# Bidirectional SSD mixer: decay exponents on 128 rows, C B masked 256 columns at a time, weighing on ScalarE

## The chip, the core and the metric

The kernel runs on one core of a Trainium2 chip. The metric is the device time of one execution in microseconds (us), lower is better. A core has TensorE (PE; matmuls into PSUM), VectorE (DVE), ScalarE (ACT), GpSimd (POOL) and SyncE (SP, which here issues the loads).

## What is computed

One encoder layer on 256 tokens of width 2048, in float32: a mixer, a gated conv feed-forward part, and a gated per-layer embedding, each between RMS norms. The mixer projects the normed input once with w_in into z, xbc, dt and u; the pooling half maps u; the SSD half is a bidirectional state-space scan with 16 heads in two groups, chunks of 128 tokens, and B and C of 128 states for each group. The change lies in the scan:

```python
dt = softplus(dt_raw + dt_bias)          # a column of its own for each direction
acum = cumsum(dt * a)
decay = exp(where(causal, acum[l] - acum[s], -inf))
cb = C[l] . B[s]                         # for each group
y_diag = einsum(cb, decay, xs * dt)      # within a chunk of 128
y_off = C . h_in * exp(acum)             # from the other chunk
y = y_fwd + flip(y_bwd) + xs * d_skip
```

## The kernel before, in words

Tokens form two chunks of 128 (t = 0, 1). Matrix products keep float32 accuracy by splitting each operand into a high half, a rounded copy (line 149, ScalarE, for weights), and a low half, the rest (line 150, VectorE); each product is then three fp32r matmuls: high-high, high-low, low-high. Weights come from HBM as 1 MB tiles (`raw`, 3 buffers); `whi` and `wlo` (lines 145 and 146) have 5 buffers each for the halves.

The mixer runs in this order. The projection onto dt and u (`dtu`, lines 399 to 436). Then three slabs of xbc, 512 columns each, feature-major: `xbc(2)` (B and C), `xbc(0)` and `xbc(1)` (xs), four units of w_in each. After a slab: scaling by rows (`times_rows`, line 367), a convolution of five taps (`conv`, lines 378 and 384), and SiLU (lines 598 and 600). Then z, token-major, eight units of two 128-row tiles (line 683). Then the norm of y, and the output projection `wo`.

The small work of the scan is laid between the units: `work` is a list of job lists, and `aside()` takes one list after every unit (lines 189 to 194). The tile framework then puts the instructions into the engines' queues when the program is built, by its own reckoning of what is ready, with the source's order as priority. So a queue's order is fixed before the run, but isn't the source's word for word. Each engine takes its queue in order.

The jobs that matter here:

- `seg_sums` (line 521): cumulative sums of the decays by a matmul, and from them `seg_w` and `seg_x`, two pages of which 64 rows are used: heads and a selection of ones, so that a matmul gives acum[l] - acum[s] for four heads at once. Half of the rows are filled early (lines 446 and 448), half here (532 and 533).
- `seg(i)`, i = 0 to 7 (line 535): two matmuls, one for each direction, `seg_w` (64 rows, 128 columns) by `seg_x` (64 rows, 512 columns), into two `misc` PSUM tiles; ScalarE copies one (541), VectorE takes the minimum of the two (542), ScalarE the exponential (543), into `ee[t]`. Where s <= l the minimum picks the forward exponent, elsewhere the backward one.
- `cb(cv, g)` (line 572): C B for one group, 256x256 in four blocks; the two diagonal blocks are multiplied by 0.25 and two masks into `cbm[0]` and `cbm[1]` (581, VectorE), the off-diagonal ones by 0.25 into `cbm[2]` (583, ScalarE).
- `weigh(t, g)` (line 603): w = cbm[0] dt_fwd + cbm[1] dt_bwd for the eight heads of a group: the second product by GpSimd (606), the first one and the sum by VectorE, 128 columns an instruction (611); then `ee` is multiplied by w (615). `w` is a `mid` tile (1024 columns, 3 buffers, shared with the tiles of the convolution).
- `far` and `skip` (lines 620, 625): xs scaled by the decays to the chunk's end, and xs times d_skip, on GpSimd.
- `mix(t, g)` (line 629): the part from the other chunk (`yo`, with `cbm[2]`), and eight matmuls of `ee` by `xs` (`yd`), into y. It needs the weighed `ee`.
- `pool_map` (line 559): matmuls of the pooling half, fp32, 128 rows.

`page` is a pool of 13 tiles of 2048 columns that nearly everything large shares (normed input: four pages until z ends; `ee` 2, `cath1`, `catl1`, `cbm`, `xs`, `y`, `xd` 2, and so on); a tile waits until a page is free. `misc` is two PSUM banks, `main` six.

Of the kernel before, what the change touches and what calls it, by code (L numbers as in the profile page):

```python
# [11 lines left out]
F32 = mybir.dt.float32  # L12
F32R = mybir.dt.float32r
AF = mybir.ActivationFunctionType
ALU = mybir.AluOpType

P = 128
L = 256
# [3 lines left out]
H = 16  # L22
# [29 lines left out]
def build(nc, a, out):  # L52
# [5 lines left out]
    with tile.TileContext(nc) as tc, \  # L58
# [11 lines left out]
        def page(name, dtype=F32):  # L70
            return gp.tile([P, 2048], dtype, tag="pg", bufs=13, name=name)

        def mid(name, dtype=F32):
            return gp.tile([P, 1024], dtype, tag="mid", bufs=3, name=name)

        def tiny(name, n=2):
            return sp.tile([P, n], F32, tag="tiny", bufs=40, name=name)
# [4 lines left out]
        def misc(name):  # L82
            return pc.tile([P, 512], F32, tag="misc", name=name)

        def mm(o, lhsT, rhs, start, stop):
            nc.tensor.matmul(o, lhsT, rhs, start=start, stop=stop, skip_group_check=True)  # L86
# [28 lines left out]
        def load(dst, src, ahead=False):  # L115

            with tc.issue_after(last["dma"]) if last and not ahead else nullcontext():
                return ins(nc.sync.dma_start(dst, src))
# [11 lines left out]
        mask = small[:, 80:592].rearrange("p (m f) -> p m f", m=4)  # L130

        low, among, four = small[:64, 592:593], small[:64, 593:597], small[:64, 597:601]
# [210 lines left out]
        def row_rstd(name, src):  # L343

            r = []
            for t in range(2):
                q = tiny(f"{name}q{t}", 1)
                junk = page(f"{name}j{t}")
                nc.scalar.activation(junk, src[t], AF.Square, accum_out=q)
                r.append(rms(f"{name}{t}", [q], 1.0 / D))  # L350
            return r
# [86 lines left out]
        with tc.issue_after(half[0]), tc.issue_after(half[1]):  # L438
            xs_ = [page(f"x{t}") for t in range(2)]
            for t in range(2):  # L440
                load(xs_[t], x[t * P:(t + 1) * P, :])
            rx = row_rstd("rx", xs_)
            seg_w = page("seg_w", F32R)[:64, :].rearrange("p (a q s) -> p a q s", a=4, q=4)
            seg_x = page("seg_x", F32R)[:64, :].rearrange("p (a i l) -> p a i l", a=4, i=4)
            for a_ in range(4):
                nc.scalar.activation(seg_w[:32, a_], four[:32].unsqueeze(2).to_broadcast([32, 4, P]), AF.Copy,
                                     scale=-1.0)
                nc.scalar.copy(seg_x[32:, a_], among[32:].unsqueeze(2).to_broadcast([32, 4, P]))
            aneg = ep.tile([P, 32], F32, name="aneg")
            nc.scalar.activation(aneg, alog, AF.Exp)  # L450
            nc.gpsimd.tensor_scalar(aneg, aneg, -1.0, None, op0=ALU.mult)


            pt = page("pt")[:, :512].rearrange("p (k t) -> p k t", k=2)
            load(pt, a["p_t"])
            half_up = cp.tile([P, 1], F32, name="half_up")
            nc.gpsimd.memset(half_up, 0.5)
            pth = cp.tile([P, 2, L], F32R, name="pth")
            ptl = cp.tile([P, 2, L], F32R, name="ptl")
            nc.scalar.copy(pth, pt)  # L460
            nc.vector.tensor_sub(ptl, pt, pth.bitcast(F32))
# [8 lines left out]
        dt = ep.tile([P, 2, 32], F32, name="dt")  # L470
        ut = page("u")
        for t in range(2):
# [3 lines left out]
                                    op0=ALU.mult)  # L476
# [44 lines left out]
        def seg_sums():  # L521

            cps = misc("cps")
            for a_ in range(4):
                mm(cps[:64, a_ * P:(a_ + 1) * P], da4[:, a_ // 2, a_ % 2].rearrange("p r h -> p (r h)"),
                   mask[:, 3 * (a_ % 2), :], True, True)
            hi, c = page("seg_h", F32R)[:64, :512], page("seg_c")[:64, :512]
            nc.scalar.copy(hi, cps[:64, :])
            nc.vector.scalar_tensor_tensor(c, hi.bitcast(F32), low, cps[:64, :], op0=ALU.mult, op1=ALU.add)
            c4 = c.rearrange("p (a l) -> p a l", a=4)  # L530
            for i in range(4):
                nc.scalar.activation(seg_x[:32, :, i, :], c4[:32], AF.Copy, scale=among[:32, i:i + 1])
                nc.scalar.activation(seg_w[32:, :, i, :], c4[32:], AF.Copy, scale=four[32:, i:i + 1])

        def seg(i):
            t, q = divmod(i, 4)
# [29 lines left out]
                put(cat(8 + 2 * g + d), ps[:, d * L:(d + 1) * L], vec(V_PS + 2 * g + d))  # L566


        cbm = page("cbm")[:, :1536].rearrange("p (m g s l) -> p m g s l", m=3, g=2, s=2)
        xs = page("xs")  # L570

        def cb(cv, g):
            ps = misc(f"cb{g}")
            for s in range(2):
                mm(ps[:, s * L:(s + 1) * L], cv[:, g * L + s * P:g * L + (s + 1) * P],
                   cv[:, (2 + g) * L:(3 + g) * L], True, True)
            for s in range(2):
                dg = ps[:, s * L + s * P:s * L + (s + 1) * P]
                og = ps[:, s * L + (1 - s) * P:s * L + (2 - s) * P]
                for d in range(2):  # L580
                    nc.vector.scalar_tensor_tensor(cbm[:, d, g, s, :], dg, 0.25, mask[:, d, :],
                                                   op0=ALU.mult, op1=ALU.mult)
                nc.scalar.activation(cbm[:, 2, g, s, :], og, AF.Copy, scale=0.25)

        def xs_turn(cv, slab):
            for t in range(2):
# [15 lines left out]

        def weigh(t, g):

            w = mid(f"w{t}{g}")
            nc.gpsimd.tensor_tensor(w.rearrange("p (h l) -> p h l", h=8),
                                    cbm[:, 1, g, t, :].unsqueeze(1).to_broadcast([P, 8, P]),
                                    dt[:, t, H + 8 * g:H + 8 * g + 8].unsqueeze(2).to_broadcast([P, 8, P]),
                                    op=ALU.mult)
            for h in range(8):  # L610
                nc.vector.scalar_tensor_tensor(w[:, h * P:(h + 1) * P], cbm[:, 0, g, t, :],
                                               dt[:, t, 8 * g + h:8 * g + h + 1], w[:, h * P:(h + 1) * P],
                                               op0=ALU.mult, op1=ALU.add)
            es = ee[t][:, g * 1024:(g + 1) * 1024]
            nc.vector.tensor_mul(es, es, w)

        def by_head(ap_, n=H):
            return ap_.rearrange("p (h c) -> p h c", h=n)
# [10 lines left out]
        def mix(t, g):  # L629
            c0 = t * 1024 + g * 512  # L630
            s = 1 - t
            po = misc(f"yo{t}{g}")
            mm(po, cbm[:, 2, g, s, :], xd[s][:, g * 512:(g + 1) * 512], True, True)
            tm = mid(f"ym{t}{g}")[:, :512]
            nc.vector.tensor_tensor(by_head(tm, 8), by_head(po, 8),
                                    dec[:, 2 + s, 8 * g:8 * g + 8].unsqueeze(2).to_broadcast([P, 8, 64]), op=ALU.mult)
            nc.gpsimd.tensor_add(y[:, c0:c0 + 512], y[:, c0:c0 + 512], tm)
            pd = misc(f"yd{t}{g}")
            for h in range(8):
                mm(pd[:, h * 64:(h + 1) * 64], ee[t][:, (8 * g + h) * P:(8 * g + h + 1) * P],  # L640
                   xs[:, c0 + h * 64:c0 + (h + 1) * 64], True, True)
            nc.vector.tensor_add(y[:, c0:c0 + 512], y[:, c0:c0 + 512], pd)

        def job(f, *args):
            return lambda: f(*args)

        xd = {}
        work.extend([
            [],
            [job(pool_mix, 0), job(pool_mix, 1)],  # L650
            [job(pool_mix, 2), job(pool_mix, 3), job(decays), job(seg_sums)],
            [job(seg, 0), job(seg, 1)],
        ])
# [1 line left out]
        work.extend([  # L655
            [job(seg, 2), job(pool_map, 0), job(pool_map, 1)],
            [job(cb, bc, 0), job(cb, bc, 1), job(seg, 3)],
            [job(seg, 4), job(weigh, 0, 0), job(pool_map, 2)],
            [job(seg, 5), job(weigh, 0, 1), job(pool_map, 3)],
        ])  # L660
        xa = xbc(0)
        work.extend([
            [job(seg, 6)],
            [job(seg, 7), job(weigh, 1, 0)],
            [job(xs_turn, xa, 0), job(weigh, 1, 1)],
            [],
        ])
        xb = xbc(1)
# [1 line left out]


        work.extend([
            [],
            [],
            [],
            [job(xs_turn, xb, 1)],
            [job(far, 1), job(skip, 0), job(far, 0), job(skip, 1)],
            [job(mix, 0, 0)],
            [job(mix, 0, 1), job(mix, 1, 0)],
            [job(mix, 1, 1)],  # L680
# [89 lines left out]
        h = [page(f"h{t}") for t in range(2)]  # L770
# [116 lines left out]
        for half in range(2):  # L887
# [10 lines left out]
            for t in range(2):  # L898
                for n, (o, c0) in enumerate(columns(acc[t])):
# [6 lines left out]
                    if end:  # L906
# [3 lines left out]
                                                   op0=ALU.add, op1=ALU.mult)  # L910
                    q = tiny(f"gq{t}{half}{n}", 1)
# [60 lines left out]
```

## Time and profile before

| | us |
|---|---|
| median of 3 runs | 1136.15 (1134.97 to 1136.28) |
| the profiled execution | 1134.8 |
| its span, first to last instruction | 1132.7 |
| busy: TensorE | 1115.6 (98%) |
| busy: VectorE | 801.1 (71%) |
| busy: ScalarE | 612.0 (54%) |
| busy: GpSimd | 79.7 (7%) |

The granted TensorE clock is 0.997 of full speed over the span. The profile is one execution. Its page gives busy times, the chain of work that ended last, and groups of instructions; views of the trace give instructions in order of time, waits, and busy times by window. In the trace xbc(2) begins at 52.4 us, xbc(0) ends about 117, z begins at 148.1 and the output projection at 203.8. A row's shape `64*128 64x512` reads: the loaded operand has 64 rows and 128 columns, the moving one 64 rows and 512 columns. Records of matmuls overlap, since they are pipelined: the spacing of their starts is the rate, not their duration. Tile names in rows are those of the program without numbers: `xb_0l` is a low half of an xbc slab's weights, `z_1h` a high half of z's.

### The profile page before, as it was taken

How to read it: one execution, taken by the hardware profiler on the slowest of the kernel's cores; microseconds unless marked ns; L12 is line 12 of the kernel's file. 1: busy time of each engine (PE TensorE's matmuls, PEld its weight loads, DVE VectorE, ACT ScalarE, POOL GpSimd, SP SyncE). 2: the span in 40 equal slices, each digit the busy share in tenths (PEclk: the TensorE clock that was granted, in tenths of full speed). 3: DMA queues.
4: the chain of work that ended last, by engine and by line, in shares of the span. 5: the costliest groups of instructions: out<-in, count | busy, mean ns of one | idle time of the engine just before them, and what ended most of it. 6: DMA issues, size and time to landing. Idle time of an engine off the chain costs nothing.

```text
span 1132.7 us, 15349 instructions
## 1 busy us (share of the span) xinstructions
PE 1115.6 (98%) x6049; PEld 969.4 (86%) x6049; DVE 801.1 (71%) x1067; ACT 612.0 (54%) x837; POOL 79.7 (7%) x91
## 2 busy tenths in 40 slices
PE   9999999999999999999999999999999999999996
PEld 9998888888788888888888888888888888887885
DVE  6659995754866665665756666668988998898574
ACT  6846543554664545454544545454665666667462
POOL 0201105200110000000000000000000000002001
PEclk9999999999999999999999999999999999999998
DMA  9942276556456555655555555657466656665752
GB/s 357 377 148 75 90 260 227 175 177 197 147 185 193 192 194 192 196 187 186 186 187 188 188 191 193 196 190 227 153 221 217 204 173 222 189 210 159 230 179 74
DMA packets 129591, 219.03 MB, mean 193 GB/s; under 512 B 3696, under 2 KB 96752, under 8 KB 128624
## 3 DMA queue, kind: packets, MB, share of 16 engines
q1 hardware_dynamic: 129232, 217.70, 58.5%
q8 instruction: 47, 0.77, 0.3%
q10 hardware_dynamic: 288, 0.36, 0.1%
q14 instruction: 24, 0.20, 0.0%
HBM read 215.95 MB, written 2.10 MB: 192 GB/s over the span
## 4 chain that ended last, share of the span: by engine, by line
PE 94%; DVE 3%; ACT 1%; POOL 1%; issue 1%; DMA 0%; POOLq 0%; DVEq 0%; ACTq 0%
PE va L86 22%; PE ga L86 21%; PE dna L86 17%; PE woa L86 8%; PE gt L86 7%; PE xbc L86 5%; PE dtu L86 4%; PE z L86 4%; PE dns L86 3%; DVE h L751 1%; PE pw L86 1%; PE yd L86 0%; PE seg L86 0%; DMA dtur<-w_in 0%; PE mx L86 0%
## 5 line engine op out<-in xcount | busy, mean ns | idle before, releaser
L86 PE MATMUL ga<-wox,ug_0h 128*128 128x512 f32 x352 | 88.4, 391 | 0.0
L86 PE MATMUL ga<-wox,ug_1h 128*128 128x512 f32 x352 | 87.6, 390 | 0.0
L86 PE MATMUL va<-wox,uv_0h 128*128 128x512 f32 x352 | 87.5, 391 | 0.0
L86 PE MATMUL va<-wox,uv_1h 128*128 128x512 f32 x352 | 86.9, 389 | 0.0
L86 PEld LDWEIGHTS va<-wox,uv_1h 128*128 128x128 f32 x352 | 66.1, 188 | 13.7
L86 PEld LDWEIGHTS ga<-wox,ug_1h 128*128 128x128 f32 x352 | 65.8, 188 | 13.6
L86 PEld LDWEIGHTS va<-wox,uv_0h 128*128 128x128 f32 x352 | 64.7, 188 | 12.5
L86 PEld LDWEIGHTS ga<-wox,ug_0h 128*128 128x128 f32 x352 | 64.5, 188 | 12.2
L86 PE MATMUL dna<-dn_0h,hs 128*128 128x512 f32 x248 | 74.7, 389 | 0.0
L86 PE MATMUL dna<-dn_1h,hs 128*128 128x512 f32 x248 | 74.6, 389 | 0.0
L792 POOL TENSOR_TENSOR fc<-fc,rfb 128x1024 f32<-128x1024 f32 x11 | 26.7, 2426 | 439.1 <-ACT fc L791 439.1
L86 PEld LDWEIGHTS dna<-dn_0h,hs 128*128 128x128 f32 x248 | 46.5, 188 | 9.7
L86 PEld LDWEIGHTS dna<-dn_1h,hs 128*128 128x128 f32 x248 | 46.6, 188 | 9.7
L86 PE MATMUL ga<-wox,ug_1l 128*128 128x256 f32 x352 | 50.3, 284 | 0.0
L86 PE MATMUL ga<-wox,ug_0l 128*128 128x256 f32 x352 | 49.5, 283 | 0.0
L86 PE MATMUL va<-wox,uv_1l 128*128 128x256 f32 x352 | 49.4, 283 | 0.0
L86 PE MATMUL va<-wox,uv_0l 128*128 128x256 f32 x352 | 49.2, 283 | 0.0
L86 PEld LDWEIGHTS ga<-wox,ug_0l 128*128 128x128 f32 x352 | 46.8, 191 | 1.7
L86 PEld LDWEIGHTS va<-wox,uv_0l 128*128 128x128 f32 x352 | 46.7, 191 | 1.7
L86 PEld LDWEIGHTS ga<-wox,ug_1l 128*128 128x128 f32 x352 | 45.7, 192 | 0.2
L384 DVE SCALAR_TENSOR_TENSOR fc<-gr,vt,fc 128x255 f32<-128x255 f32 x88 | 40.3, 481 | 7.7 <-ACT fc L378 7.0
L86 PEld LDWEIGHTS va<-wox,uv_1l 128*128 128x128 f32 x352 | 45.4, 192 | 0.0
(1078 smaller groups left out, 2800.9 us busy)
## 6 DMA issues: line engine op xcount, KB each, us to landing
dn0r<-w_ffn_down SPq DMA_DIRECT2D x22, 1024.0 KB, 5.6
dn1r<-w_ffn_down SPq DMA_DIRECT2D x22, 1024.0 KB, 5.6
zr<-w_in SPq DMA_DIRECT2D x8, 1024.0 KB, 5.4
wo0r<-w_out SPq DMA_DIRECT2D x8, 1024.0 KB, 5.7
wo1r<-w_out SPq DMA_DIRECT2D x8, 1024.0 KB, 5.5
gt0r<-w_ple_gate SPq DMA_DIRECT2D x8, 1024.0 KB, 6.3
gt1r<-w_ple_gate SPq DMA_DIRECT2D x8, 1024.0 KB, 5.5
dtur<-w_in SPq DMA_DIRECT2D x14, 528.0 KB, 8.9
```

The lines of the kernel that those rows point to most:

```text
L86: nc.tensor.matmul(o, lhsT, rhs, start=start, stop=stop, skip_group_check=True)
L384: nc.vector.scalar_tensor_tensor(o[:, lo:hi], i[:, lo + d:hi + d], vec(wcol + j * wstep + f), o[:, lo:hi], op0=ALU.mult, op1=ALU.add)
L751: nc.vector.scalar_tensor_tensor(h[t][:, s], mg[t][:, s], r[t], h[t][:, s], op0=ALU.mult, op1=ALU.add)
L792: nc.gpsimd.tensor_tensor(cv.rearrange("p (f t) -> p f t", f=4), cv.rearrange("p (f t) -> p f t", f=4), rfb.unsqueeze(1).to_broadcast([P, ...
```

## The change

Three edits in the scan. First, `seg_w` and `seg_x` keep all 128 rows: two GpSimd memsets set rows 64 to 127 to zero, and the seg matmuls, whose source line doesn't change, contract over 128 rows. Second, `cb` copies the whole 256 columns for each s (512 in all) by one ScalarE instruction, scaled by 0.25, into `cbs`, and VectorE multiplies a diagonal block by both masks at once, 256 columns an instruction; the off-diagonal blocks are read from `cbs`. Third, `weigh` makes both products on ScalarE, one activation for each head and direction with dt as its scale, into the two halves of a page; VectorE adds the halves and multiplies `ee`. The four weighings move: the first from xbc(0) to the third unit of xbc(1), the others from xbc(0) and xbc(1) into z.

```diff
-            seg_w = page("seg_w", F32R)[:64, :].rearrange("p (a q s) -> p a q s", a=4, q=4)
-            seg_x = page("seg_x", F32R)[:64, :].rearrange("p (a i l) -> p a i l", a=4, i=4)
+            seg_w, seg_x = page("seg_w", F32R), page("seg_x", F32R)
+            for blank in (seg_w, seg_x):
+                nc.gpsimd.memset(blank[64:, :].bitcast(F32), 0.0)
+            seg_w = seg_w.rearrange("p (a q s) -> p a q s", a=4, q=4)
+            seg_x = seg_x.rearrange("p (a i l) -> p a i l", a=4, i=4)
...
-                nc.scalar.copy(seg_x[32:, a_], among[32:].unsqueeze(2).to_broadcast([32, 4, P]))
+                nc.scalar.copy(seg_x[32:64, a_], among[32:].unsqueeze(2).to_broadcast([32, 4, P]))
...
-                nc.scalar.activation(seg_w[32:, :, i, :], c4[32:], AF.Copy, scale=four[32:, i:i + 1])
+                nc.scalar.activation(seg_w[32:64, :, i, :], c4[32:], AF.Copy, scale=four[32:, i:i + 1])
...
-        cbm = page("cbm")[:, :1536].rearrange("p (m g s l) -> p m g s l", m=3, g=2, s=2)
+        cbm = page("cbm")
+        cbs = cbm[:, 1024:].rearrange("p (g s l) -> p g s l", g=2, s=2)
+        cbm = cbm[:, :1024].rearrange("p (m g s l) -> p m g s l", m=2, g=2, s=2)
...
+            nc.scalar.activation(cbs[:, g].rearrange("p s l -> p (s l)"), ps, AF.Copy, scale=0.25)
             for s in range(2):
-                dg = ps[:, s * L + s * P:s * L + (s + 1) * P]
-                og = ps[:, s * L + (1 - s) * P:s * L + (2 - s) * P]
-                for d in range(2):
-                    nc.vector.scalar_tensor_tensor(cbm[:, d, g, s, :], dg, 0.25, mask[:, d, :],
-                                                   op0=ALU.mult, op1=ALU.mult)
-                nc.scalar.activation(cbm[:, 2, g, s, :], og, AF.Copy, scale=0.25)
+                nc.vector.tensor_mul(cbm[:, :, g, s, :], mask[:, :2, :],
+                                     cbs[:, g, s, s * P:(s + 1) * P].unsqueeze(1).to_broadcast([P, 2, P]))
...
-            w = mid(f"w{t}{g}")
-            nc.gpsimd.tensor_tensor(w.rearrange("p (h l) -> p h l", h=8),
-                                    cbm[:, 1, g, t, :].unsqueeze(1).to_broadcast([P, 8, P]),
-                                    dt[:, t, H + 8 * g:H + 8 * g + 8].unsqueeze(2).to_broadcast([P, 8, P]),
-                                    op=ALU.mult)
-            for h in range(8):
-                nc.vector.scalar_tensor_tensor(w[:, h * P:(h + 1) * P], cbm[:, 0, g, t, :],
-                                               dt[:, t, 8 * g + h:8 * g + h + 1], w[:, h * P:(h + 1) * P],
-                                               op0=ALU.mult, op1=ALU.add)
+            w = page(f"w{t}{g}")
+            for d in range(2):
+                for h in range(8):
+                    nc.scalar.activation(w[:, d * 1024 + h * P:d * 1024 + (h + 1) * P], cbm[:, d, g, t, :], AF.Copy,
+                                         scale=dt[:, t, d * H + 8 * g + h:d * H + 8 * g + h + 1])
+            nc.vector.tensor_add(w[:, :1024], w[:, :1024], w[:, 1024:])
             es = ee[t][:, g * 1024:(g + 1) * 1024]
-            nc.vector.tensor_mul(es, es, w)
+            nc.vector.tensor_mul(es, es, w[:, :1024])
...
-            mm(po, cbm[:, 2, g, s, :], xd[s][:, g * 512:(g + 1) * 512], True, True)
+            mm(po, cbs[:, g, s, (1 - s) * P:(2 - s) * P], xd[s][:, g * 512:(g + 1) * 512], True, True)
...
-            [job(seg, 4), job(weigh, 0, 0), job(pool_map, 2)],
-            [job(seg, 5), job(weigh, 0, 1), job(pool_map, 3)],
+            [job(seg, 4), job(pool_map, 2)],
+            [job(seg, 5), job(pool_map, 3)],
...
-            [job(seg, 7), job(weigh, 1, 0)],
-            [job(xs_turn, xa, 0), job(weigh, 1, 1)],
+            [job(seg, 7)],
+            [job(xs_turn, xa, 0), job(weigh, 0, 0)],
...
+            [job(weigh, 0, 1)],
             [],
-            [],
-            [],
+            [job(weigh, 1, 0)],
             [job(xs_turn, xb, 1)],
-            [job(far, 1), job(skip, 0), job(far, 0), job(skip, 1)],
+            [job(weigh, 1, 1), job(far, 1), job(skip, 0), job(far, 0), job(skip, 1)],
```

## The prediction

> **What bounds the kernel now.** I read the page first, then the windows over the stretch that the change touches (the mixer, 74 to 204 us), then TensorE's waits there, then the chain, and last the instructions of TensorE, VectorE, ScalarE and GpSimd in order of time.
>
> ```profile
> span 1132.7 us, 15349 instructions
> PE 1115.6 (98%) x6049; PEld 969.4 (86%) x6049; DVE 801.1 (71%) x1067; ACT 612.0 (54%) x837; POOL 79.7 (7%) x91
> ```
>
> TensorE is busy for 98% of the span, so the kernel gains only where TensorE waits or where its instructions take longer than their columns ask. In the windows (busy us of PE, PEld, DVE, ACT and POOL after the stretch and its length) the crowded engine beside TensorE is VectorE:
>
> ```profile
> core 0: us, PE busy (x) PEld busy (x) DVE busy (x) ACT busy (x) POOL busy (x), PEclk, DMA share, GB/s
> ...
> 100.00:123.00 23.00, 23.00 (x157) 20.70 (x156) 22.30 (x47) 13.21 (x23) 3.75 (x2) 1.00 0.42 138
> 123.00:137.00 14.00, 11.46 (x87) 10.16 (x85) 13.70 (x26) 8.27 (x12) 3.84 (x2) 1.00 0.24 76
> 137.00:148.30 11.30, 11.30 (x93) 11.30 (x94) 11.30 (x17) 3.16 (x4) 0.00 (x0) 1.00 0.49 149
> 148.30:203.80 55.50, 55.31 (x273) 45.40 (x273) 39.53 (x47) 24.42 (x30) 16.45 (x9) 1.00 0.68 235
> ```
>
> VectorE is full from 100 to 148 us (47.3 of 48.3), ScalarE is not (24.6), and from 148 to 204 us ScalarE has 24.4 of 55.5 us. TensorE falls short in one stretch, 123 to 137 us. Its waits say on what:
>
> ```profile
> PE xbc L86 <- DVE xb_0l L150: 2.0, 1, 2.0
> PE seg L86 <- ACT seg_x L532: 0.7, 1, 0.7
> PE xbc L86 <- DVE xb_1l L150: 0.5, 1, 0.5
> ```
>
> Two waits, 2.5 us together, are for low halves of w_in tiles (line 150) that VectorE makes late. The third, for ScalarE's spreading of the exponents (line 532), the change leaves alone. The chain (start, duration, what) shows the later half and gives the undisturbed rates of TensorE:
>
> ```profile
> 52.62 11.52 PE xbc L86 x96
> ...
> 119.19 1.73 PE pw L86 x8
> ...
> 135.79 1.15 DVE xb_0l L150
> ...
> 170.94 10.90 PE z L86 x48
> ...
> 202.04 1.73 PE yd L86 x16
> ```
>
> A 256-column matmul on 128 rows takes 11.52 / 96 = 0.120 us, a 512-column one 10.90 / 48 = 0.227 us.
>
> **Part 1, decay exponents on 128 rows.** The 16 matmuls of `seg` have 64 rows. Here, above, is a `pool_map`, whose 8 records have 128 rows, between xbc matmuls, and below it a pair of seg matmuls in the same surroundings (start, duration):
>
> ```profile
> 118.90 0.28 PE L86 MATMUL xbc<-hnh,xb_0l 128*128 128x256 f32 x1
> 119.02 1.89 PE L86 MATMUL pw<-mixt,poolw 128*128 128x256 f32 x8
> 120.56 0.47 PE L86 MATMUL xbc<-hnh,xb_0h 128*128 128x256 f32 x1
> ...
> 120.99 0.28 PE L86 MATMUL xbc<-hnh,xb_0l 128*128 128x256 f32 x1
> ...
> 125.30 0.28 PE L86 MATMUL xbc<-hnh,xb_1l 128*128 128x256 f32 x1
> 125.51 0.73 PE L86 MATMUL seg<-seg_x,seg_w 64*128 64x512 f32 x2
> 126.17 0.39 PE L86 MATMUL xbc<-hnh,xb_0h 128*128 128x256 f32 x1
> 126.39 0.28 PE L86 MATMUL xbc<-hnl,xb_0h 128*128 128x256 f32 x1
> 126.51 0.28 PE L86 MATMUL xbc<-hnh,xb_0l 128*128 128x256 f32 x1
> ```
>
> From 118.90 to 120.99 us there are three xbc and the pw: 3 x 0.120 + 1.73 = 2.09, and 2.09 passed: the 128-row insert costs nothing beyond itself. From 125.30 to 126.51 there are three xbc and two 512-column ones: 3 x 0.120 + 2 x 0.227 = 0.81, and 1.21 passed: 0.39 us are lost going into the 64-row shape and out of it, at the start (0.21 to the seg instead of 0.12), behind the last seg and at the second xbc (0.22 instead of 0.12). A seg that stands alone loses as much:
>
> ```profile
> 86.18 0.28 PE L86 MATMUL xbc<-hnh,xb_1l 128*128 128x256 f32 x1
> 86.39 0.49 PE L86 MATMUL seg<-seg_x,seg_w 64*128 64x512 f32 x1
> ...
> 87.15 0.28 PE L86 MATMUL xbc<-hnh,xb_1l 128*128 128x256 f32 x1
> ```
>
> From 86.18 to 87.15 is 0.97, and three xbc with one seg need 0.59: 0.38 lost. The seg matmuls (below: count, shortest/median/longest ns, first and last start) stand in 10 such groups, 6 pairs and 4 single ones:
>
> ```profile
> L86 PE MATMUL seg<-seg_x,seg_w x16: 393/492/497, 84.8 to 130.0; 64*128 64x512 f32 x16
> ```
>
> With 128 rows the shape is that of the neighbours. The gain lies between nothing (if it isn't the rows) and 10 x 0.39 = 3.9 us. I take 3.8, since the first group's entry lies under the wait for `seg_x`.
>
> The Trainium skill speaks against this part: TensorEngine Tiling, Overview, holds that a contraction of 64 rows or fewer leaves the array half used and can gain up to 2x as two row tiles. By it the padding gives an overlap away. The trace doesn't bear it out here: both matmuls of a pair lie on rows 0 to 63, and the pair took 0.39 us more than its columns, not less. The fourth rival prices it.
>
> The zeros are two GpSimd memsets of 64x2048.
>
> ```profile
> 0.75 0.20 POOL masks.py:197 MEMSET ident<- 128x128 f32 x1
> ...
> 41.15 0.56 POOL L326 TENSOR_TENSOR rx1r<-rx1m,mhalf 128x1 f32<-128x1 f32 x1
> ```
>
> At most 16 times the width of the one above, 3.2 us each, at least 0.2 each. Queued on GpSimd behind them at worst is the reciprocal root `rx1r`, which then ends at 41.7 + 6.4 = 48.1 us; its users follow the first projection's last matmul, shortly before 52.62, where xbc starts. Cost nothing; without that cover up to 6.4 us.
>
> **Part 2, the weighing leaves VectorE and GpSimd.** Before, each of four weighings costs VectorE 8 instructions of line 611 and a product, with a GpSimd product ahead of it. Two run in the 100 to 123 us window, two from 127.94 on. Below are VectorE's groups from 117 to 137 us (count, busy us, mean ns), from the end of xbc(0) to the late half, and the product of GpSimd among them:
>
> ```profile
> L611 DVE SCALAR_TENSOR_TENSOR w<-cbm,dt,w 128x128 f32<-128x128 f32 x8 | 3.3, 471 | 0.0
> L150 DVE TENSOR_TENSOR xb_1l<-xb1r,xb_1h 128x1024 fp32r<-128x1024 f32 x1 | 2.6, 2629 | 0.0
> L150 DVE TENSOR_TENSOR xb_0l<-xb1r,xb_0h 128x1024 fp32r<-128x1024 f32 x2 | 2.4, 1212 | 0.0
> ...
> L615 DVE TENSOR_TENSOR E<-E,w 128x1024 f32<-128x1024 f32 x1 | 1.2, 1214 | 0.0
> ```
> ```profile
> 127.94 1.90 POOL L606 TENSOR_TENSOR w<-cbm,dt 128x1024 f32<-128x1024 f32 x1 [22.34 <-DVE cv L384]
> ```
>
> The low half `xb_1l`, whose lateness is the 0.5 us wait, took 2.63 us beside GpSimd's product, where the same instruction alone takes 1.21: 1.4 us of contention. After the change the stretch before the 135.79 half loses that 1.4 and the 3.3 us of line 611: 4.7 us. What must be covered is 2.5 us of waits and the 1.2 us by which TensorE comes sooner, since three of the ten groups lie behind the end of xbc(0) at 117, from which this VectorE work starts: 3.7. In addition the two weighings before 117 us go, which lets earlier low halves run sooner. What comes in is one weighing's add and product, 2 x 1.2 us, needed only by the `yd` matmuls late in z. So both waits go: 2.5 us, and with the late one a slower restart:
>
> ```profile
> 133.95 1.03 PE L589 MATMUL xt<-ident,cv 128*128 128x128 f32 x8
> 136.99 0.39 PE L86 MATMUL xbc<-hnh,xb_0l 128*128 128x256 f32 x1 [2.00 <-DVE xb_0l L150]
> 137.21 0.28 PE L86 MATMUL xbc<-hnh,xb_0h 128*128 128x256 f32 x1
> ```
>
> 137.21 - 136.99 is 0.22 in place of 0.12: 0.1. Next late after that is only TensorE's own work: from 137 to 204 us it is busy for all but 0.2.
>
> **Part 3, 64 multiplications on ScalarE.** No row has one of this form (128 wide, from SBUF, scale from a column). The nearest two:
>
> ```profile
> 148.81 2.08 ACT L378 ACTIVATE cv<-xr,vt 128x256 f32<-128x256 f32 x4 [2.19 <-DVE xr L367]
> ...
> 103.43 0.28 ACT L583 ACTIVATE cbm<-cb 128x128 f32<-128x128 f32 x1 [0.22 <-DVE cbm L581]
> ```
>
> Twice as wide with scale and bias from columns: 2.08 / 4 = 0.52. The same width with a constant scale: 0.28. I take 0.30, next to the row of equal width: 4.8 us a weighing (4.5 to 8.3). Three lie in z, 14.4 us (13.4 to 25.0), on top of ScalarE's 24.4 of 55.5 us. Queued behind them on ScalarE are the high halves of w_in (line 149); for these there are five buffers (line 145) and a z tile takes TensorE 12 x 0.227 = 2.7 us, so they run up to four tiles, 10.9 us, ahead, and one weighing of at most 8.3 us doesn't reach TensorE. The last weighing, issued after the fifth of eight z units (about 182 us), must be done when the last yd starts at 202: 8.3 + 2.4 us fit. The one in xbc(1) has the same cover (four tiles of 24 x 0.120 = 2.9 us). Cost nothing; what a failure costs is the third rival.
>
> The Trainium skill speaks against this part too: ScalarE: Activation LUTs, Rules for kernel authors, sends multiplications and additions to VectorE. By it the weighing is more engine time than before, which I grant; it changes the end only where ScalarE comes to bound, which is the third rival.
>
> **Part 4, the rest.** The C B masking: 8 VectorE instructions and 4 ScalarE ones become 4 and 2 wider ones, in a place where TensorE has 23.0 of 23.0; nothing. The `w` pages (13 in the pool): from z on 11 are held, so two weighings fit, and `far(0)` waits for the last to be freed; its first user is the seventh z unit. Nothing. No DMA is added; loads only come sooner with freed buffers.
>
> **Sum.** 3.8 + 2.5 + 0.1 = 6.4 us. The profiled execution took 1134.8 us (span 1132.7), 0.1% under the median of the runs, 1136.15. It would come to 1128.4, the median to 1129.8. About 0.2%, 2.3 us, is what a measurement of this kernel can tell from no change.
>
> **Rivals.**
> 1. The loss at seg isn't the rows but the 512 columns or the new output, and stays: only the waits go, 2.6 us, 1133.6. Against it: xbc to pw changed output too, at no loss. For it: no fp32r insert of 512 columns on 128 rows stands among xbc in this trace. If the padding did not reach the instruction it would be the same.
> 2. VectorE still ends last at 137: what follows the end of xbc(0) (117 us) doesn't shorten, and TensorE, sooner there, waits longer. Then only the seven groups before it count: 2.7 us, 1133.4. For it: VectorE's 13.70 of 14.00. Against: 4.7 us leave, 3.7 are asked, a margin of 1.0 us.
> 3. Slower: ScalarE's queue takes the three weighings of z in one run, as all their inputs are ready from 104 us, and the high halves stand behind them: 48 x 0.52 = 25.0 us, less 10.9 of lead, 14.1 of wait, net +7.7: 1143.8. It ends slower than before once the run is over 10.9 + 6.4 = 17.3 us. For it: queue order is fixed when the program is built. Against: two pages hold two weighings at most, and the high halves of early tiles come first in the source.
> 4. Two 64-row matmuls overlapped, and the padding ends that: half of 16 x 0.227, 1.8 us, comes back, a gain of 4.6, 1131.6. Against it stand the 1.21 us of the pair above.
>
> **How the numbers follow.** The forecast 0.72, the first rival 0.06, the second 0.12, the third 0.05, the fourth 0.02, small new waits that eat the gain 0.03. Faster takes the forecast, the second and fourth rivals and half of the first: 0.89; the third is slower, 0.05; the rest same, 0.06. Upward the range reaches to the first two rivals, 1133.6. Downward: the 0.7 us wait for `seg_x` going too, and the 1.2 us by which the lowest run lies under the median: 1127.9.
>
> **What would show it.** Right: seg rows of 128x512 with 0.12 us from the xbc before and after (0.81 for the stretch above, not 1.21); no wait of TensorE on line 150 between 100 and 150 us; z starting some 6 us sooner, near 142; ScalarE near 39 us in z with TensorE still full. Wrong: seg groups that still take 1.2; a TensorE wait on line 149 or 150, or on `E`, in z; ScalarE rows of the weighing over 0.5 us.

## The result, and the profile after

| | before | after |
|---|---|---|
| median | 1136.18 us (1134.77 to 1138.08, 20 runs) | 1134.24 us (1133.46 to 1136.93, 20 runs) |
| profiled execution | 1134.8 us | 1136.76 us |
| its span | 1132.7 us | 1135.0 us |

The ratio of after to before is 0.9987, 95% interval 0.9981 to 0.9993: some 1.5 us less (0.8 to 2.2), where 6.4 were forecast, and outside the range. The profiled execution of after is one of the two slowest of its 20, so its profile shows more loss than its median has; which part of it is not the change is worked out below.

TensorE's waits between 50 and 210 us in the profile of after:

```profile
PE z L86 <- DVE z_1l L150: 2.5, 1, 2.5
...
```

Both waits for `xb` halves are gone, as forecast, and a new one of 2.5 us has come, for a low half of a z tile, which the prediction named as what would show it wrong. The windows, with the columns of those of before:

```profile
...
123.00:137.00 14.00, 14.00 (x115) 13.82 (x114) 12.18 (x20) 8.27 (x11) 0.00 (x0) 1.00 0.45 145
137.00:148.30 11.30, 11.30 (x82) 10.65 (x81) 6.00 (x8) 10.27 (x29) 0.00 (x0) 1.00 0.30 102
148.30:203.80 55.50, 52.77 (x250) 42.56 (x250) 46.68 (x50) 34.92 (x70) 16.63 (x8) 0.97 0.61 209
```

TensorE is full from 123 to 148 us, where before it had 11.46 of 14.00. It falls short in the last window (52.77 of 55.50), and there the granted clock is 0.97. The chain gives the marks; after first, then before (start, duration):

```profile
54.38 11.52 PE xbc L86 x96
...
204.64 10.51 PE woa L86 x46
```
```profile
203.77 11.42 PE woa L86 x50
```

And the first z matmuls of after and of before:

```profile
144.47 0.63 PE L86 MATMUL z<-z_0h,hnh 128*128 128x512 f32 x2
```
```profile
148.12 0.63 PE L86 MATMUL z<-z_0h,hnh 128*128 128x512 f32 x2
```

From the start of xbc to that of z, before took 148.12 - 52.62 = 95.5 us and after 144.47 - 54.38 = 90.1: 5.4 less. From z to the output projection, before took 203.77 - 148.12 = 55.65 and after 60.17: 4.5 more. The span of after is 2.3 us longer all the same: 0.9 less from these two, 1.76 more at the start (xbc begins at 54.38, not 52.62) and 1.43 more behind 1036 us. Neither of the last two is the change: kernels with the same memsets began xbc anywhere from 52.5 us (e12, below) to 54.8 (e5), one without them (e7) at 53.2, and behind 1036 us both kernels are the same program. The second is told of in the last section.

So the first half of the forecast came, 5.4 of 6.4 us, and z gave most of it back. TensorE around the new wait:

```profile
156.30 0.90 PE L86 MATMUL z<-z_1l,hnh 128*128 128x512 f32 x2 [2.54 <-DVE z_1l L150]
156.99 1.05 PE L86 MATMUL z<-z_1h,hnl 128*128 128x512 f32 x2
157.85 1.05 PE L86 MATMUL z<-z_1l,hnh 128*128 128x512 f32 x2
```

Two matmuls that are 0.45 us from pair to pair elsewhere are 0.85 apart after the wait: half rate. The granted clock (third figure from the right) says for how long, 3.41 us:

```profile
...
156.70:160.11 3.41, 3.41 (x10) 2.65 (x9) 3.41 (x4) 3.41 (x13) 0.00 (x0) 0.50 0.78 246
```

The 4.5 us are the wait, 2.54, and about 2.0 of restart and slow matmuls. What VectorE did meanwhile:

```profile
143.96 0.69 DVE L367 TENSOR_TENSOR xr<-xbc,rxb 128x512 f32<-128x512 f32 x1 [3.68 <-PE xbc L86]
144.71 1.23 DVE L612 TENSOR_TENSOR w<-w 128x1024 f32<-128x1024 f32 x1
145.85 0.68 DVE L367 TENSOR_TENSOR xr<-xbc,rxb 128x512 f32<-128x512 f32 x1
146.45 1.22 DVE L614 TENSOR_TENSOR E<-E,w 128x1024 f32<-128x1024 f32 x1
147.58 6.39 DVE L384 SCALAR_TENSOR_TENSOR cv<-xr,vt,cv 128x254 f32<-128x254 f32 x16
153.90 1.21 DVE L612 TENSOR_TENSOR w<-w 128x1024 f32<-128x1024 f32 x1
155.03 1.21 DVE L150 TENSOR_TENSOR z_1l<-zr,z_1h 128x1024 fp32r<-128x1024 f32 x1
```

VectorE had nothing to do for 3.68 us, until the last xbc matmul. Then seven pieces of work stand in its queue, back to back, and the half that TensorE wants is the last of them: the convolution of `xb`, and among it three pieces of the weighing (w00's add and product, w01's add), 1.14 us each from start to start. ScalarE's queue shows what stands ahead of its high half; the split of this z unit comes in the source behind w01.

```profile
137.97 1.05 ACT L149 CAST z_0h<-zr 128x1024 fp32r<-128x1024 f32 x1 [1.75 <-issue]
...
139.89 5.07 ACT L610 ACTIVATE w<-cbm,dt 128x128 f32<-128x128 f32 x17
145.02 1.09 ACT L378 ACTIVATE cv<-xr,vt 128x256 f32<-128x256 f32 x2
146.02 0.98 ACT L610 ACTIVATE w<-cbm,dt 128x128 f32<-128x128 f32 x3
146.90 1.08 ACT L378 ACTIVATE cv<-xr,vt 128x256 f32<-128x256 f32 x2
147.88 3.61 ACT L610 ACTIVATE w<-cbm,dt 128x128 f32<-128x128 f32 x12
151.40 1.04 ACT L149 CAST z_1h<-zr 128x1024 fp32r<-128x1024 f32 x1
```

Between the two high halves of one unit, 13.4 us apart, ScalarE makes both w00 and w01, 32 multiplications, and the convolution's products. Which of the two queues ends last is a question for experiments.

### The profile page after: what moved, and what is told of

It is laid out like the page before. It is cut to its first block, busy times and chain, and to the rows that moved or that the text cites. A ratio compares the mean times of both kernels' runs of the same rounds, so it can differ in the third digit from the quotient of the medians.

```text
span 1135.0 us, 15377 instructions
## 1 busy us (share of the span) xinstructions
PE 1117.3 (98%) x6049; PEld 973.6 (86%) x6049; DVE 798.7 (70%) x1035; ACT 630.3 (56%) x899; POOL 74.4 (7%) x89
## 4 chain that ended last, share of the span: by engine, by line
PE 93%; DVE 3%; ACT 2%; issue 1%; POOL 1%; DMA 0%; POOLq 0%; DVEq 0%; ACTq 0%
PE va L86 22%; PE ga L86 21%; PE dna L86 17%; PE woa L86 8%; PE gt L86 7%; PE xbc L86 5%; PE dtu L86 4%; PE z L86 3%; PE dns L86 3%; DVE h L750 1%; PE pw L86 1%; DVE cv L384 1%; PE yd L86 0%; ACT w L610 0%; PE seg L86 0%
```

## The experiments

Every median stands beside runs of the kernel before on the same chip, and the ratio is to these. "Changed" means the kernel after.

**e1, the rows alone.** The first edit of the change, on the kernel before: 

```diff
+            seg_w, seg_x = page("seg_w", F32R), page("seg_x", F32R)
+            for blank in (seg_w, seg_x):
+                nc.gpsimd.memset(blank[64:, :].bitcast(F32), 0.0)
```

> The kernel before with only the seg operands on 128 rows (and the two memsets). Theory: the ten seg groups shrink by 0.38 us each; VectorE still makes the two late halves, so the waits of 2.5 us stay and may grow by up to 1.2 us, since TensorE comes sooner: 2.5 to 3.8 us under the kernel before, seg groups at 0.81 and 0.59 us. Rival, the memsets cost the start of the run 1.8 us: 0.7 to 2.0 us under it, with xbc starting near 54.4 us. Rival, the rows don't matter: no change.

1135.06 us against 1136.05, ratio 0.9988 (0.9979 to 0.9998): less than expected. The time is in the range of the memset rival too, but xbc starts at 52.67 us, not near 54.4. TensorE's waits in its profile say where the gain went:

```profile
PE xbc L86 <- DVE xb_0l L150: 2.0, 1, 2.0
PE xbc L86 <- DVE xb_1l L150: 1.1, 1, 1.1
PE seg L86 <- DVE catl L186: 1.0, 1, 1.0
```

4.1 us of waits on VectorE in place of 2.5: with VectorE as full as before, TensorE that comes sooner waits longer. In this execution half clock follows the 2.0 us wait as well (granted clock 0.88 from 137 to 148.3 us), and from xbc to z it takes 96.1 us, not less than before. The longer waits are the mechanism of the second rival, in the kernel that lacks the second half of the change.

**e2, the changed kernel with 64 rows.** The same edit taken back from the changed kernel.

> The changed kernel with the seg operands back on 64 rows and no memset. Theory: the seg groups take 1.2 us again and the wait in z (2.5 us, and a lower clock behind it) stays: 2 to 4 us over the changed kernel, so 0 to 2.5 us over the kernel before. Rival, the changed kernel loses at its start by the memsets: only 2 us over the changed kernel, about the time of the kernel before, with xbc starting near 52.6 us.

1137.26 us, ratio 1.0012 (1.0003 to 1.0021), 3.0 over the changed kernel's median; from xbc to z it takes 92.7 us, 2.6 more. The z wait is still 2.5 us. So the rows are worth more where VectorE is relieved than alone.

**e3, the weighing as before, at the new places.** GpSimd's product and VectorE's multiply-adds in place of lines 607 to 612 of the changed kernel.

> The changed kernel with the weighing of before (GpSimd and VectorE) at the new places. Theory, ScalarE's run of 32 multiplications ahead of the second high half of z's unit 1 makes the wait in z: that wait is gone, 5 to 6.5 us under the kernel before (1129.7 to 1131.2). Rival, the work that the weighing brings VectorE in z is enough for the wait: VectorE has more of it here (8 x 0.27 us for an add of 1.2), so the wait stays at 2.5 us or more, 0 to 2 us under the kernel before.

1136.58 us, ratio 1.0004 (0.9995 to 1.0012): the time is not the theory's. But the changed kernel's wait, in the second z unit, is gone: with no multiplications on ScalarE, that unit's low half is made ahead of the convolution of `xb`. A wait of 4.2 us has come in the fourth unit instead, where the multiply-adds stand in VectorE's queue themselves:

```profile
141.20 1.22 DVE L150 TENSOR_TENSOR z_1l<-zr,z_1h 128x1024 fp32r<-128x1024 f32 x1 [1.12 <-ACT z_1h L149]
142.35 1.41 DVE L367 TENSOR_TENSOR xr<-xbc,rxb 128x512 f32<-128x512 f32 x2
...
161.94 3.58 DVE L613 SCALAR_TENSOR_TENSOR w<-cbm,dt,w 128x128 f32<-128x128 f32 x7
165.45 1.21 DVE L150 TENSOR_TENSOR z_1l<-zr,z_1h 128x1024 fp32r<-128x1024 f32 x1
```

So the theory had the first wait right, and the rival came near the time: the weighing's work on VectorE is enough for a wait of its own.

**e4, the changed kernel with its weighings placed anew.**

```diff
-            [job(seg, 6)],
+            [job(seg, 6), job(weigh, 0, 0)],
...
-            [job(xs_turn, xa, 0), job(weigh, 0, 0)],
+            [job(xs_turn, xa, 0)],
...
-            [job(weigh, 0, 1)],
+            [],
             [],
-            [job(weigh, 1, 0)],
-            [job(xs_turn, xb, 1)],
+            [job(weigh, 0, 1)],
+            [job(xs_turn, xb, 1), job(weigh, 1, 0)],
```

> The changed kernel, with the first weighing in the first unit of xbc(1) and the next two two units later in z, so that no more than 7 multiplications stand ahead of that high half. ScalarE and VectorE do the same work as in the changed kernel. Theory: no wait of TensorE on z_1l, clock in z at 1.00, 5.5 to 6.5 us under the kernel before (1129.7 to 1130.7). Rival, the amount of work on VectorE or ScalarE in z makes the wait: it stays, near 1134.

1129.38 us (1129.04 to 1131.11, 5 runs), ratio 0.9946 (0.9934 to 0.9958): better than both kernels. No wait in z, and the window full:

```profile
148.30:203.80 55.50, 55.31 (x273) 45.38 (x272) 42.76 (x47) 31.31 (x59) 21.40 (x14) 1.00 0.61 209
```

VectorE's queue has turned around, as in e3. The low half stands ahead of the convolution, and 7 multiplications stand ahead of its high half on ScalarE, where the changed kernel has 32:

```profile
141.74 1.23 DVE L150 TENSOR_TENSOR z_1l<-zr,z_1h 128x1024 fp32r<-128x1024 f32 x1 [2.73 <-ACT z_1h L149]
142.88 1.28 DVE L367 TENSOR_TENSOR xr<-xbc,rxb 128x512 f32<-128x512 f32 x2
144.30 6.14 DVE L384 SCALAR_TENSOR_TENSOR cv<-xr,vt,cv 128x254 f32<-128x254 f32 x15
```

In the 12.28 us from 142.88 on VectorE is busy for 12.11 and ScalarE for all, as in the changed kernel at this place (12.22 and 12.23 of 12.28); only the order differs.

**e5, the ScalarE weighing at the places of before.** Is it the place alone, then?

```diff
-            [job(seg, 4), job(pool_map, 2)],
-            [job(seg, 5), job(pool_map, 3)],
+            [job(seg, 4), job(weigh, 0, 0), job(pool_map, 2)],
+            [job(seg, 5), job(weigh, 0, 1), job(pool_map, 3)],
...
+            [job(seg, 7), job(weigh, 1, 0)],
+            [job(xs_turn, xa, 0), job(weigh, 1, 1)],
```

> The changed kernel's ScalarE weighing and 128 rows, with the four weighings where the kernel before has them (three in the xbc part, one in the unit where xa is turned). Theory (the place decides: two weighings and the conv between two splits of z are what made TensorE wait): no wait of TensorE in z; in the xbc part ScalarE, 13.3 of 23.0 us busy at 100 to 123 us, takes 4.8 us for each weighing and VectorE only 2.4, so no wait for xb_0l either; time about that of the run with the weighings placed anew, 1129 to 1131 us. Rival (a weighing of 4.8 us on ScalarE holds back a split wherever it stands): a wait of 1 to 3 us for an xb or xa tile's half, with half clock behind it, 1132 to 1135 us.

1140.33 us, ratio 1.0034 (1.0021 to 1.0048): slower than before, and the theory missed. The rival's wait came, with half clock behind it (granted clock 0.70 from 137 to 148.3 us), but the loss is larger than it said. ScalarE is full there (14.00 of 14.00 us from 123 to 137), with all four weighings between 121 and 146 us, and a high half of `xb` stands behind three of them:

```profile
138.00 1.85 ACT L610 ACTIVATE w<-cbm,dt 128x128 f32<-128x128 f32 x6
139.75 1.04 ACT L149 CAST xb_1h<-xb1r 128x1024 fp32r<-128x1024 f32 x1
```
```profile
140.84 0.58 PE L86 MATMUL xbc<-hnh,xb_1h 128*128 128x256 f32 x1 [2.96 <-ACT xb_1h L149]
```

**e8, the weighing as before, at e4's places.**

> The weighings at the new better places, with 128 rows, but done as in the kernel before: GpSimd's product and VectorE's eight multiply-adds. Theory (the place decides, on whichever engine): VectorE, 42.8 of 55.5 us busy in z, takes some 2.4 us more for each of three weighings plus what GpSimd costs it, which still fits; waits of TensorE in z and xbc of at most 0.5 us in all, 1129 to 1131 us. Rival (VectorE has no room, so that ScalarE is needed for the gain): waits of 1.5 us and more with half clock behind them, 1132 to 1136 us.

1141.72 us, ratio 1.0049 (1.0037 to 1.0061). The rival held, and more than held. TensorE waits 8.0 us for low halves, 6.4 of them behind one weighing:

```profile
170.13 8.76 DVE L613 SCALAR_TENSOR_TENSOR w<-cbm,dt,w 128x128 f32<-128x128 f32 x8
178.82 1.21 DVE L150 TENSOR_TENSOR z_0l<-zr,z_0h 128x1024 fp32r<-128x1024 f32 x1
```

Eight multiply-adds took 2.18 us at 131.77 with GpSimd idle, 3.8 beside a GpSimd product of 1.9, and 8.76 here, beside GpSimd's products of `xd` and `y`. So engine and place belong together: the old places suit VectorE's weighing, e4's suit ScalarE's, and either at the other's places is slower than before.

**e7, e4 with 64 rows.** What the rows are worth where nothing else waits.

> The kernel with the weighings placed anew, with the decay exponents on 64 rows as before. If the loss at the ten seg groups is 0.39 us each and nothing else hides or eats it: 3.5 to 4.1 us slower than the run with the weighings placed anew (1129.4), so 1132.9 to 1133.5. Rival (rows are worth only the 1.2 us that they gave alone): 1130.4 to 1131.

1132.12 us, ratio 0.9962 (0.9951 to 0.9974), 2.7 over e4 by the medians (1.8 by the ratios) and so less than the 3.8 of the forecast. The stretches that hold a `seg` pair, nine xbc and a `pool_map` tell where it shrank, e4 first, then e7 (chain; start, duration):

```profile
107.90 0.47 PE seg L86 x2
...
111.44 4.67 PE xbc L86 x39
```
```profile
109.51 0.66 PE seg L86 x2
...
113.16 4.67 PE xbc L86 x39
```

3.54 us with 128 rows, 3.65 with 64: a gain of 0.11, not 0.39. In e4 the `pool_map` now waits, and its weight load says for what:

```profile
109.45 1.59 PEld L86 LDWEIGHTS pw<-mixt,poolw 128*128 128x128 f32 x8 [0.23 <-ACT E L544]
```

It writes to one of the two `misc` PSUM tiles, and that is free only when ScalarE has copied the seg sums out of it (`E`, line 544). With 64 rows TensorE came 0.39 us later and the copy was done.

**e6 and e9, half of e4 each.** e6 moves only the z weighings later and leaves w00; e9 moves only w00 earlier and leaves the others.

> The changed kernel with only the z weighings moved: the first two slots later (third slot of z), the second one slot later (fourth), w00 left in the third unit of the second xbc half. Theory (w00's run, the conv and w01 together stand ahead of the second split): ScalarE's cast z_1h comes near 146.7 us in place of 151.4, but VectorE's conv of 6.4 us still waits for ScalarE's conv products behind w00, and z_1l comes only 1.2 to 1.7 us sooner: a wait of 0.8 to 1.4 us is left, and the kernel is 1 to 2.5 us faster than the changed one, 1131.5 to 1133. If w01 alone is the cause: no wait, 1129 to 1130.5. If w00 alone is the cause: a wait of 2 us or more stays, 1133.5 to 1134.5.

> The changed kernel with only w00 moved, to the first unit of the second xbc half; the three z weighings stay where the change has them. Theory (a second weighing run in front of the second split is what is too much; either of the two, with the conv and the E product on VectorE, leaves some 1.2 to 1.5 us of wait, as moving the z weighings did): a wait of z for z_1l of 1.0 to 1.6 us, clock full after it, 1131 to 1132.2 us. If w00 alone is the cause: a wait of at most 0.3 us, 1129 to 1130. If w01 alone is the cause: 2 us or more, 1133.5 to 1134.5.

e6: 1131.44 us, ratio 0.9956 (0.9944 to 0.9968); e9: 1131.38 us, ratio 0.9970 (0.9960 to 0.9981). The chips differ (the kernel before has 1136.22 us beside e6 and 1135.12 beside e9), but from z to the output projection both take 57.5 us. e9 is what the theory had, e6 just outside it, and neither w00 nor w01 alone is the cause. The wait of e6:

```profile
153.51 0.73 PE L86 MATMUL z<-z_1l,hnh 128*128 128x512 f32 x2 [1.44 <-DVE z_1l L150]
```

e9 has 1.45 us at the same place. In both the clock stays full behind it.

**e10, half of the multiplications.** ScalarE makes only the forward direction (the backward one is left out), VectorE's work is the same:

```diff
-            for d in range(2):
+            for d in range(1):
...
-            nc.vector.tensor_add(w[:, :1024], w[:, :1024], w[:, 1024:])
+            nc.vector.tensor_add(w[:, :1024], w[:, :1024], w[:, :1024])
```

> The changed kernel with eight ScalarE multiplications in each weighing in place of 16 (the backward direction is left out; VectorE adds the forward half to itself, so its work is the same). ScalarE's two runs ahead of z_1h are then 4.8 us in all in place of 9.6. Theory (the delay is passed on: ScalarE's runs make the conv on VectorE late, and VectorE's conv of 6.4 us with an E product stands ahead of z_1l): ScalarE's cast z_1h comes some 4 to 5 us sooner, z_1l only 1 to 2 us sooner, a wait of 0.8 to 2 us stays, 1131 to 1133.5 us. Rival (ScalarE's lateness alone): no wait, 1129 to 1130 us.

1133.17 us, ratio 0.9984 (0.9976 to 0.9993). ScalarE's high half starts at 142.85 us, 8.5 sooner than in the changed kernel (6.8 when counted from the start of z), and TensorE waits 2.1 us all the same:

```profile
142.85 1.04 ACT L149 CAST z_1h<-zr 128x1024 fp32r<-128x1024 f32 x1
```
```profile
152.83 1.21 DVE L150 TENSOR_TENSOR z_1l<-zr,z_1h 128x1024 fp32r<-128x1024 f32 x1
```

That settles which queue ends last: VectorE's. Two pieces of weighing are still ahead of the half behind the last xbc matmul, and the first `xr` starts 0.8 us late behind w00's product. At run time ScalarE's runs hold up next to nothing. They go with the order of VectorE's queue: with none or 7 multiplications ahead of this high half (e3, e4) its low half stands ahead of the convolution, with 16 or more (the changed kernel, e6, e9 to e12) behind it. That the order was set by them when the program was built fits this, but no run shows the framework's reckoning.

**e11 and e12, doses.** e6 with one and with two more VectorE additions behind w00's, on a half of `w` that isn't read again:

```diff
+            for _ in range(1 if (t, g) == (0, 0) else 0):
+                nc.vector.tensor_add(w[:, 1024:], w[:, 1024:], w[:, 1024:])
```

> The kernel with the z weighings later (which had a wait of 1.44 us for z_1l and a full clock after it), with one more VectorE addition of 1.14 us behind w00's, on a half of w that is not read again, so that it stands ahead of that z_1l. It measures the price of a longer wait. The wait should be 2.4 to 2.7 us. If a wait costs only itself: 1.1 us more than without, 1132.3 to 1132.9. If a wait of this length also brings the half clock that followed the 2.54 us in the changed kernel: 1.1 plus 1.9, 1134 to 1134.8.

> As the run before it with two such additions: a wait of 3.5 to 3.9 us. If a wait costs only itself: 1133.4 to 1134. If the half clock follows: 1135.2 to 1136.

The first is e11, the second e12:

```profile
154.78 0.73 PE L86 MATMUL z<-z_1l,hnh 128*128 128x512 f32 x2 [2.57 <-DVE z_1l L150]
155.35 0.63 PE L86 MATMUL z<-z_1h,hnl 128*128 128x512 f32 x2
```
```profile
155.57 1.09 PE L86 MATMUL z<-z_1l,hnh 128*128 128x512 f32 x2 [3.71 <-DVE z_1l L150]
156.46 1.05 PE L86 MATMUL z<-z_1h,hnl 128*128 128x512 f32 x2
```

Waits of 2.57 and 3.71 us, after e6's 1.44: each piece of 1.14 us adds 1.14. The times are 1134.72 us, ratio 0.9990 (0.9981 to 0.9999), and 1135.97 us, 1.0004 (0.9995 to 1.0012). The first dose cost 3.3 us by the medians (3.9 by the ratios; e6 ran on another chip), much more than itself, as the half clock would have it; but in e11's profiled execution, one of its fastest at 1133.65, the matmuls after the wait ran at full rate, and the half rate came after a later wait (below). So a wait's own time is shown; what follows it can differ between executions (last section).

## Why the prediction was wrong, point by point

**Part 1** (128 rows) was right in kind: the pair at 131.64 us in the profile of after stands 0.12 from its neighbours, and from the xbc before it to the second behind it 0.82 us pass, where 0.81 was forecast and 1.21 was before. The size was off: 3.8 forecast, 2.5 measured, both as the stretch from xbc to z (90.1 us in e4, 92.6 in e7) and as 2.7 between the medians. "10 x 0.39" took every group for one whose loss is on the path. Two lie so close ahead of a `pool_map` that it now waits for its PSUM tile (0.6 us together), a third gains only 0.2, and some of the single ones lose up to 0.2 with 128 rows too. I had asked what the loss is, not what is late next when it goes. e2 and e7 leave no room for the first and the fourth rival, since the rows alone gave some 2.5 us from xbc to z in both.

**Part 2** held: no wait for an `xb` half. e7, which has it without the rows, goes from xbc to z 2.9 us faster than before, against the 2.6 of the forecast. The price of the memsets was in its bounds (1.81 us each) and their cover held. The sentence that failed stands here all the same: what comes in is "one weighing's add and product, 2 x 1.2 us, needed only by the `yd` matmuls late in z". When a result is needed says nothing about what stands behind the work. In VectorE's queue three such pieces stood ahead of the second low half of the second z unit. Part 4 (the C B masking) was put at nothing, and no run has it alone.

**Part 3** is the step that made the forecast wrong. The multiplication cost 0.30 us as taken (16 in 4.79, e6), but "one weighing of at most 8.3 us doesn't reach TensorE" looked at one weighing and at ScalarE alone. Two weighings lie between the two halves of one unit, and the engine that ends last is VectorE. The third rival had the right place, `z` halves behind the weighings, and was dismissed because "the high halves of early tiles come first in the source". They don't: w01 is in the list after the first z unit, and the splits of the second unit come behind it. The numbers of the VectorE queue close. Without the three pieces the half would be done at 156.24 - 3.41 = 152.83 us, and TensorE wanted it at 156.30 - 2.54 = 153.76: 0.9 us of slack. Two pieces give 2.28 - 0.9 = 1.4 (e6 1.44, e9 1.45), three 2.5 (2.54, from which the slack is worked out, and e11 2.57), four 3.6 (e12 3.71).

**The share of busy time** misled me: ScalarE's 24.4 of 55.5 us and VectorE's 39.5 are means over all of z. In the profile of after VectorE is busy for 12.22 of the 12.28 us between 143.96 and 156.24. The Trainium skill warns of this: Perfetto Trace Analysis, Optimization Strategy, says that a kernel can have regimes with different most contended engines and that gaps are to be looked for within the regime. The trace agrees, and e4 adds that even there the busy time isn't the measure: it is nearly the same in e4 (12.11), which has no wait.

**The sum.** 5.4 us arrived at the start of z. The wait with its restart costs 2.9 (e11, whose wait is as long and whose clock stayed full, took that much more than before from z to the output projection), and 1.6 more where the clock halves, 4.5 in all: a gain of 2.5 us without the half clock and of 0.9 with it. The measured 1.5 lies between. That e4 comes to 1129.38, next to the 1129.8 forecast, is partly chance: its stretch from xbc to z is 5.4 us shorter, not 6.4, and the rest lies within its interval (4.8 to 7.5 us).

## What to carry to other kernels

A piece of work that is moved costs what stands behind it in each engine's queue, whenever its own result is needed: write out the queue from the last thing that must wait (here the last xbc matmul) to the half that TensorE asks for, and compare it with TensorE's lead. Splitting work over two engines doubles this, since the order on one can hang on what was put on the other. And when a loss on the path goes, look for the buffer that the loss had been hiding.

## What the runs showed of the hardware

The same wait has two prices. Near 1035 us all fourteen profiles hold the same wait of 2.3 us, for `gt_1l`, in a part that no kernel here changes. Before, and then after:

```profile
1035.54 0.73 PE L86 MATMUL gt<-gt_1l,dnxh 128*128 128x512 f32 x2 [2.27 <-DVE gt_1l L150]
...
1036.35 1.04 PE L336 MATMUL dnxt<-ident,h 128*128 128x128 f32 x8
```
```profile
1036.40 0.73 PE L86 MATMUL gt<-gt_1l,dnxh 128*128 128x512 f32 x2 [2.29 <-DVE gt_1l L150]
...
1037.21 1.78 PE L336 MATMUL dnxt<-ident,h 128*128 128x128 f32 x8
```

In nine of the fourteen the matmuls behind it run at half rate (granted clock 0.50) for 3.41 us, which costs 1.4 us; in five, that of before among them, they don't. Behind the z wait it was so after 2.54 us (changed kernel, e2), 3.71 (e12) and 4.16 (e3), and not after 2.57 (e11), 2.09 (e10), 1.45 (e9) and 1.44 (e6).

What decides can be read from the traces. Where a profile has several stretches of half clock, their starts lie whole numbers of steps of 3.4133 us apart: 156.696 and 1037.336 us in the profile of after (258.0 steps), 155.742 and 1036.382 in e12 (258.0), 136.278 and 1037.396 in e1 (264.0). Each lasts one step, 3.41 us, or two, 6.83 (e5, e8). So the steps of each profile can be laid out on both sides of such a stretch (in before, e6 and e7 of the one after TensorE's last work; e9 has none), and from 20 us to TensorE's last work they part the waits. Wherever TensorE waited for 2.00 us or more within one step, the clock was halved in the next (the least is e1's 2.00, before 136.278); where it was 1.96 or less (the most is e5's, for `gt_1l`), it wasn't, but for the second step of e5's stretch. The border is near 2 us and not sharp: behind the last work of before, 1.89 us without a matmul were enough. The 2.57 us of e11 fell into two steps, 0.82 and 1.75, those of before near 1035 us too, 0.38 and 1.89; the 2.54 and 2.29 of after lay in one step each. The Trainium skill, TensorE: Matmul & The Clock Gate, What's actually happening, says that the clock halves after an idle window of about 3.4 us, and that this window runs freely and doesn't start with the kernel. The traces agree on the length and on the free run: the steps are 3.4133 us and lie differently in every profile. If an idle window is one without any matmul, they don't agree: 2.00 us of waiting in one step were enough. For reading it means that one profile can differ from the next by 1.4 us at a place that nobody touched, and that a median of 20 runs of such a kernel can hold a mixture.
